# Sixteen rounds of adaLN modulation computed as row sums on VectorE in a two-layer diffusion trunk

## The chip, the cores and the metric

The kernel runs on one core of a Trainium2 chip. The metric is the device time of one execution in microseconds (us), as the median over the runs shown. Engines are named as the profile names them: PE is TensorE (its matmuls), PEld its weight loads, DVE is VectorE, ACT is ScalarE, POOL is GpSimd, and SP is SyncE, whose queue issues the loads of weights.

## The reference, cut to what matters

The model has two layers of three sub-layers each (FFN, token mixing, FFN), so six sub-layers, numbered 0 to 5 here. 128 context tokens and 256 latent tokens of width 1024 pass through all of them. Each sub-layer is modulated by three vectors of 1024 values, for each of two conditions (context and latent): a shift, a scale and a gate. These 18 vectors ("rounds") are what the change is about. A round is a 2 x 1024 by 1024 x 1024 product, with a weight of 4 MB.

```python
def trunk(x, cond, ...):
    for l in range(DEPTH):                                   # 2 layers
        m = (jax.nn.silu(cond) @ mod_w[l] + mod_b[l]).reshape(cond.shape[0], N_MOD, D_MODEL)   # 9 vectors
        g = norm_w[l]
        hf = modulate_norm(x, g[0], m[:, 0], m[:, 1])        # rms_norm(x, g) * (1 + scale) + shift
        x = x + FFN_RES * m[:, 2, None] * rms_norm(swiglu(hf, ffn_w1[l, 0], ffn_w2[l, 0]), g[1])
        hm = modulate_norm(x, g[2], m[:, 3], m[:, 4])
        out = mixer(hm)                                      # layer 0: "even", layer 1: "odd"
        x = x + m[:, 5, None] * rms_norm(out, g[3])
        hf = modulate_norm(x, g[4], m[:, 6], m[:, 7])
        x = x + FFN_RES * m[:, 8, None] * rms_norm(swiglu(hf, ffn_w1[l, 1], ffn_w2[l, 1]), g[5])
```

## The kernel before, in words

**Weights.** All weights of projections and all modulation weights form one stream of units of 128 x 2048 float32 (1 MB), in an order that `plan` (L1312) writes out. `load_upto` (L113) issues them on SP's queue into four buffers, `raw` (RAW_BUFS, L31). A weight unit consists of two halves. `prep` (L121) splits each half exactly into two float32r parts, `whi` (a copy on ACT, L150) and `wlo` (a subtraction on DVE, L153). After the second half's split the unit's `raw` buffer is given back and the next unit of the stream is loaded into it (L160 to L162). Three split halves exist at a time (HALF_BUFS), and `half` (L176) prepares two halves ahead of the one that TensorE uses. Every product is three matmuls (`mm3`, L456 to L458).

**An FFN** (`ffn`, L590) takes 22 units `w1` (each two halves of 24 matmuls over 384 columns), evaluates SiLU and the product (`gate_up`, L619 to L621, L442, L443) after each, and then runs `down` (L462) with 11 units `w2` (22 chunks of 18 matmuls over 512 columns). `down` ends token tile by token tile. At the boundary to the next sub-layer (`rest`, L548) the last tile's residual, norm, transposition and modulation run on DVE and ACT, while TensorE starts the next projection with the first two tiles (`early`, then the transposes of tile 2, then `late`). Between `order_begin` and `order_end` all engines issue in program order. Only the projections and the attention of the two mixers lie outside.

**Modulation.** The first two rounds are computed at the start (`start`, L723), in both kernels in the same way. Of the other 16:

- Ten rounds run on VectorE (`mod_dve`, L223). A unit holds 256 rows of the weight, with the contraction on the partitions. Four "pieces" per unit (two blocks of 128 rows by two conditions) multiply 1024 outputs by a scalar per partition and add them to `macc` (L241, L243). After the fourth unit TensorE sums over the partitions with a vector of ones (L253, 8 matmuls). The row result goes through DVE and two transposes (L295) into vectors, or, for a gate, through DRAM to all partitions.
- Six rounds run on TensorE (`mod_pe`, L198), 8 matmuls of 256 columns for each unit (L211). For five of them, the gates of sub-layers 1 to 5, three units are the "fill" that `rest` emits at the boundary ahead of the sub-layer (L549, L550), and the fourth comes a little later. The sixth, the scale of sub-layer 2, runs inside the even mixer.

The pieces wait in a list. `emit_pieces` (L265) emits two of them after each half of `w1` (L716). In `down` it divides what is left over the chunks (L487). MOD_PLAN (L1292) says which rounds are computed in which sub-layer and how many of their units lie among the first projection's, and `spread` (L1304) places them. `macc` has one buffer, which also serves as a spare pair of weight halves at each boundary (L166).

Of the kernel before, what the change touches and what calls it, by code (L numbers as in the profile page):

```python
# [16 lines left out]
ALU = mybir.AluOpType  # L17
# [19 lines left out]
class Trunk:  # L37
    def __init__(self, ctx, tc, io):
# [19 lines left out]
        self.mbT = const("mbT", [P, 6, 2, KC])  # L58
        nc.gpsimd.dma_start(self.mbT, io["mod_bT"])
        self.sel = const("sel", [P, 2])  # L60
# [6 lines left out]
        self.ones = const("ones", [P, 2, 32])  # L67
        nc.vector.memset(self.ones, 0.0)
        for c in range(2):
            nc.vector.memset(self.ones[:, c, c : c + 1], 1.0)  # L70
        self.xh = self.cp.tile([P, KC, TOK], F32R, tag="xh", name="xh")
        self.xl = self.cp.tile([P, KC, TOK], F32R, tag="xl", name="xl")
        self.gates, self.shift, self.scale = {}, {}, {}

# [117 lines left out]

    def mod_begin(self, r, bank):
        if r % 3 == 2:
            self.mod_aux = self.sp.tile([P, 512], F32, tag="maux", name=self.name("maux"), bufs=1)
            self.nc.sync.dma_start(self.mod_aux, self.io["mod_aux"][r // 3])

    def mod_pe(self, key, bank):  # L198
        """One unit of a round on the tensor engine, in four column groups."""
        _, r, u = key  # L200
        i = self.use(key)
        self.load_upto(i)
        raw, _ = self.raw.pop(i)
        self.load_upto(i + RAW_BUFS)
        if u == 0:
            self.mod_begin(r, bank)
            self.mod_ps = self.psum(bank)
        for kk in range(2):
            k = 2 * u + kk
            for g in range(4):  # L210
                self.nc.tensor.matmul(  # L211
                    self.mod_ps[32 * g : 32 * g + 32, 0:256], self.csT[:, k, :],
                    raw[:, kk * D + 256 * g : kk * D + 256 * (g + 1)],
                    start=(k == 0), stop=(k == KC - 1),
                )

    def mod_unit(self, key, bank):
        self.mod_pe(key, bank)
        if key[2] == 3:
            self.mod_rows(key[1])  # L220
            self.mod_finish(key[1], bank)

    def mod_dve(self, key):  # L223
# [3 lines left out]
        i = self.index[key]  # L227

        def piece(kk, c):
            def run():  # L230
                if kk == c == 0:
                    self.use(key)
                    self.load_upto(i)
                    if u == 0:
                        self.mod_begin(r, self.dve_bank)
                        self.mod_acc = self.cp.tile([P, 2, D], F32, tag="macc", name=self.name("macc"))
                k = 2 * u + kk
                w = self.raw[i][0][:, kk * D : (kk + 1) * D]
                acc, sc = self.mod_acc[:, c, :], self.csT[:, k, c : c + 1]
                if k == 0:  # L240
                    nc.vector.tensor_scalar(acc, w, sc, None, op0=ALU.mult)  # L241
                else:
                    nc.vector.scalar_tensor_tensor(acc, w, sc, acc, op0=ALU.mult, op1=ALU.add)  # L243
                if kk == c == 1:
                    del self.raw[i]
                    self.load_upto(i + RAW_BUFS)
            return run

        def reduce():
            self.mod_ps = self.psum(self.dve_bank)  # L250
            for c in range(2):
                for g in range(4):
                    nc.tensor.matmul(  # L253
                        self.mod_ps[32 * g : 32 * g + 32, 0:256], self.ones[:, c, :],
                        self.mod_acc[:, c, 256 * g : 256 * (g + 1)], start=(c == 0), stop=(c == 1),
                    )
            self.mod_rows(r)

        def finish():
            self.mod_finish(r, self.dve_bank)  # L260

        reduce.wait, finish.wait = True, False
        return [piece(kk, c) for kk in range(2) for c in range(2)] + ([reduce, finish] if u == 3 else [])
# [14 lines left out]
    def mod_vec(self, kind):  # L278
        return self.sp.tile([P, 2, KC], F32, tag=("shift", "scale")[kind], name=self.name("mv"))

    def mod_rows(self, r):
        self.mod_row = self.sp.tile([P, 256], F32, tag="mrow", name=self.name("mrow"), bufs=1)
        if r % 3 < 2:
            self.nc.vector.tensor_copy(self.mod_row, self.mod_ps[:, 0:256])
        else:
            self.nc.vector.tensor_tensor(self.mod_row, self.mod_ps[:, 0:256], self.mod_aux[:, 0:256], ALU.add)

    def mod_finish(self, r, bank):
        nc = self.nc
        s, kind = divmod(r, 3)  # L290
        rows = self.mod_row
        if kind < 2:
            tp = self.psum(bank)
            for j in range(2):
                self.transpose(tp[:, j * P : (j + 1) * P], rows[:, j * P : (j + 1) * P])  # L295
            res = self.mod_vec(kind)
            for j in range(2):
                src = tp[:, j * P : (j + 1) * P].rearrange("p (g c) -> p c g", c=32)[:, 0:2, :]
                dst = res.rearrange("p c (g j) -> p c g j", j=2)[:, :, :, j]
                per = lambda v: v.rearrange("p (g j) -> p g j", j=2)[:, :, j].unsqueeze(1).to_broadcast([P, 2, 4])  # L300
                nc.vector.tensor_tensor(dst, src, per(self.mbT[:, s, kind, :]), ALU.add)
                if kind == 1:
                    nc.vector.tensor_tensor(dst, dst, per(self.nwT[:, s, :]), ALU.mult)
            (self.shift if kind == 0 else self.scale)[s] = res
        else:
            half = 1.0 if s in (1, 4) else 0.5
            nc.vector.scalar_tensor_tensor(rows, rows, half, self.mod_aux[:, 256:512], op0=ALU.mult, op1=ALU.mult)
            scr = self.dp.tile([2, 4, 256], F32, tag="gscr", name=self.name("gscr"), bufs=2)
            for c in range(2):
                nc.gpsimd.dma_start(scr[c], rows.rearrange("(g c) n -> g c n", c=32)[:, c, :])  # L310
            gate = self.cp.tile([P, 2, D], F32, tag="gate", name=self.name("gate"))
            nc.gpsimd.dma_start(
                gate.rearrange("p c d -> p (c d)"),
                scr.rearrange("c g n -> (c g n)").partition_broadcast(P),
            )
            self.gates[s] = gate

# [28 lines left out]
    def square_steps(self, srcs):  # L346
        """The mean of squares of two halves, the second one first, as steps; and where the sums are."""
# [10 lines left out]
    def post_steps(self, t, acc, s):  # L358
        """x += gate * rms_norm(acc): steps for the second half, for the first half, and the update."""
# [26 lines left out]
    def stat_steps(self, t):  # L386
        """xn = -2 * x * rstd(x); the factor is made good in the scale."""
# [25 lines left out]
    def evac_steps(self, t, tp, s):  # L413
        """xh + xl = xn^T * scale + shift"""
# [31 lines left out]
    def order_begin(self):  # L446
        """From here to order_end the engines issue in the order of the program."""
# [1008 lines left out]
```

## Time and profile before

| | us |
|---|---|
| runs shown | 1457.07, 1460.22, 1461.21 |
| median | 1460.22 |
| span of the profiled execution (first to last instruction) | 1456.7 |

The profile gives the span of its execution, from the first instruction to the last. What lies around the span in that execution isn't listed apart. The three runs lie 0.4 to 4.5 us above the span, the median 3.5 us. The core's mean granted TensorE clock is 0.998 of full speed. The span divides into: the start and the first FFN (0 to 309 us), the even mixer (to 480), two FFNs (to 766 and 1050), the odd mixer (to 1172) and the last FFN.

In the profile, busy time is the time in which an engine had an instruction of its own in work, and "idle before" is the time that an engine stood still just before a group, with the instruction that released it. Matmuls overlap, so the distance between starts, not the duration, is what one costs TensorE. The same holds for VectorE, whose instructions overlap by less than 0.1 us. The profile counts a float32 matmul of L211, L253 or of a sum as two instructions.

### The profile page before, as it was taken

How to read it: one execution, taken by the hardware profiler on the slowest of the kernel's cores; microseconds unless marked ns; L12 is line 12 of the kernel's file. 1: busy time of each engine (PE TensorE's matmuls, PEld its weight loads, DVE VectorE, ACT ScalarE, POOL GpSimd, SP SyncE). 2: the span in 40 equal slices, each digit the busy share in tenths (PEclk: the TensorE clock that was granted, in tenths of full speed). 3: DMA queues.
4: the chain of work that ended last, by engine and by line, in shares of the span. 5: the costliest groups of instructions: out<-in, count | busy, mean ns of one | idle time of the engine just before them, and what ended most of it. 6: DMA issues, size and time to landing. Idle time of an engine off the chain costs nothing.

```text
span 1456.7 us, 20527 instructions
## 1 busy us (share of the span) xinstructions
PE 1442.6 (99%) x8305; PEld 1304.5 (90%) x8305; DVE 901.9 (62%) x1453; ACT 612.3 (42%) x1020; POOL 29.2 (2%) x53
## 2 busy tenths in 40 slices
PE   8999999999999999999999999999999999999998
PEld 6999998879888999998889999988876799999886
DVE  5778767474776657667656576674668764444333
ACT  5433332463555633332345333323547663333332
POOL 0000000010000000000000000000100000000000
PEclk9999999999999999999999999999999999999999
DMA  9565565645543464455535454555371345333331
GB/s 372 203 229 221 186 229 203 231 159 187 189 167 145 158 225 175 174 195 200 212 116 210 182 194 177 207 199 184 117 267 73 116 163 191 116 129 131 116 116 44
DMA packets 39232, 258.91 MB, mean 178 GB/s; under 512 B 5040, under 2 KB 5120, under 8 KB 9696
## 3 DMA queue, kind: packets, MB, share of 16 engines
q1 hardware_dynamic: 36288, 244.87, 45.7%
q0 software_dynamic: 2848, 12.72, 2.5%
q8 instruction: 65, 1.06, 0.3%
q14 instruction: 31, 0.25, 0.1%
HBM read 255.29 MB, written 2.28 MB: 177 GB/s over the span
## 4 chain that ended last, share of the span: by engine, by line
PE 97%; DMA 1%; ACT 0%; DVE 0%; issue 0%; SPq 0%; DVEq 0%; ACTq 0%
PE psB L456 30%; PE psB L457 30%; PE psB L458 30%; PE psB L405 2%; PE psB L939 2%; PE psB L211 1%; PE psB L980 1%; DMA raw<-in_mod_w 1%; PE psB L253 1%; PE psB L786 0%; DMA x<-in_x_prompt 0%; PE psB L953 0%; PE psB L799 0%; ACT junk L352 0%; PE psB L1263 0%
## 5 line engine op out<-in xcount | busy, mean ns | idle before, releaser
L456 PE MATMUL psB<-xh,whi 128*128 128x384 f32 (+1 forms) x1536 | 517.6, 337 | 0.2 <-ACT xh L442 0.2
L457 PE MATMUL psB<-xl,whi 128*128 128x384 f32 (+1 forms) x1536 | 512.3, 334 | 0.2 <-DVE xl L443 0.2
L458 PE MATMUL psB<-xh,wlo 128*128 128x384 f32 (+1 forms) x1536 | 512.1, 333 | 0.0
L153 DVE TENSOR_TENSOR wlo<-raw,whi 128x1024 fp32r<-128x1024 f32 (+2 forms) x286 | 336.8, 1186 | 175.1 <-ACT whi L150 172.0
L150 ACT CAST whi<-raw 128x1024 fp32r<-128x1024 f32 (+1 forms) x275 | 286.5, 1045 | 341.8 <-PE psB L457 173.9
L456 PEld LDWEIGHTS psB<-xh,whi 128*128 128x128 f32 x1536 | 288.7, 188 | 8.7 <-issue 6.0
L457 PEld LDWEIGHTS psB<-xl,whi 128*128 128x128 f32 x1536 | 288.9, 188 | 1.1 <-DVE xl L443 0.7
L458 PEld LDWEIGHTS psB<-xh,wlo 128*128 128x128 f32 x1536 | 288.7, 188 | 0.0
L243 DVE SCALAR_TENSOR_TENSOR macc<-raw,csT,macc 128x1024 f32<-128x1024 f32 x140 | 173.8, 1279 | 0.0
L456 PE MATMUL psB<-whi,g 128*128 128x512 f32 x384 | 150.3, 391 | 0.0
L457 PE MATMUL psB<-wlo,g 128*128 128x512 f32 x384 | 149.6, 389 | 0.0
L458 PE MATMUL psB<-whi,g 128*128 128x512 f32 x384 | 149.5, 389 | 0.0
L621 DVE TENSOR_TENSOR gt<-psB,sil 128x384 f32<-128x384 f32 (+1 forms) x88 | 48.2, 548 | 131.5 <-PE psB L458 129.5
L442 ACT CAST g<-gt 128x384 fp32r<-128x384 f32 (+1 forms) x84 | 42.4, 505 | 175.8 <-DVE gt L621 175.8
L456 PEld LDWEIGHTS psB<-whi,g 128*128 128x128 f32 x384 | 72.1, 188 | 15.9 <-issue 1.2
L458 PEld LDWEIGHTS psB<-whi,g 128*128 128x128 f32 x384 | 72.1, 188 | 15.1
L457 PEld LDWEIGHTS psB<-wlo,g 128*128 128x128 f32 x384 | 72.1, 188 | 14.5
L619 ACT ACTIVATE sil<-psB 128x384 f32<-128x384 f32 (+1 forms) x88 | 42.7, 485 | 90.3 <-PE psB L458 90.3
L443 DVE TENSOR_TENSOR g<-gt,g 128x384 fp32r<-128x384 f32 (+1 forms) x84 | 46.1, 549 | 48.0 <-ACT g L442 48.0
L456 PE MATMUL psB<-g,g 128*128 128x512 f32 x120 | 46.9, 391 | 0.0
L458 PE MATMUL psB<-g,g 128*128 128x512 f32 x120 | 46.7, 390 | 0.0
L457 PE MATMUL psB<-g,g 128*128 128x512 f32 x120 | 46.7, 389 | 0.0
(229 smaller groups left out, 1461.1 us busy)
## 6 DMA issues: line engine op xcount, KB each, us to landing
raw<-in_ffn_w SPq DMA_DIRECT2D x129, 1024.0 KB, 4.8
raw<-in_mod_w SPq DMA_DIRECT2D x64, 1024.0 KB, 5.1
raw<-in_ev_in SPq DMA_DIRECT2D x10, 1024.0 KB, 5.4
m<-in_mod_first SPq DMA_DIRECT2D x8, 1024.0 KB, 13.0
gate<-gscr POOLq DMA_DIRECT2D x6, 1024.0 KB, 5.7
raw<-in_ev_out SPq DMA_DIRECT2D x4, 1024.0 KB, 4.8
raw<-in_od_out SPq DMA_DIRECT2D x4, 1024.0 KB, 5.4
bias<-in_rpb POOLq DMA_DIRECT2D x8, 384.0 KB, 4.0
```

Of the source, the lines that this page charges most:

```text
L150: nc.scalar.copy(hi, src)
L153: sub = lambda hi=hi[:, c], lo=lo[:, c], src=src[:, c]: nc.vector.tensor_tensor(lo, src, hi.bitcast(F32), ALU.subtract)
L243: nc.vector.scalar_tensor_tensor(acc, w, sc, acc, op0=ALU.mult, op1=ALU.add)
L405: self.nc.tensor.transpose(out, src, self.ident)
L442: self.nc.scalar.copy(hi, src)
L443: sub = lambda: self.nc.vector.tensor_tensor(lo, src, hi.bitcast(F32), ALU.subtract)
L456: nc.tensor.matmul(out, ah, bh, start=first, stop=False)
L457: nc.tensor.matmul(out, ah, bl, start=False, stop=False)
L458: nc.tensor.matmul(out, al, bh, start=False, stop=last)
L619: nc.scalar.activation(sil[:, :n], pg[:, :n], AF.Silu)
L621: nc.vector.tensor_tensor(gt[:, :n], pu[:, :n], sil[:, :n], ALU.mult)
L939: nc.tensor.matmul(sp[:, :384], qk(i, e, t + 1), kk(i, e)[0], start=True, stop=True)
```

## The change

The modulation weight is laid out transposed in DRAM: a unit now holds 256 outputs, with the outputs on the partitions and the 1024 contraction elements along the free axis. A piece becomes one `tensor_tensor_reduce` on VectorE: it multiplies 128 x 1024 weights by the conditioning vector, which stands on all partitions (`csB`, 1 MB for both conditions), sums along the free axis, starts from the bias and writes one column of the result vector. All 16 rounds take this way, 256 pieces in all. The sum over partitions, its row copies, the two transposes per shift or scale, and all modulation matmuls of these rounds are gone. A gate's vector takes one transpose of 16 columns, a copy, a write to DRAM and a load to all partitions (`gate_load`), which is issued behind `rest`.

`csB` lives in the buffer of `macc`. It is loaded anew in each sub-layer that computes rounds: the first time from the input with a SiLU on ScalarE, then from DRAM. The rounds are computed in the order 2 to 17: five in sub-layer 0, one in the even mixer (one piece after each half), five in sub-layer 2, four in sub-layer 3, none in 4, one in 5. Nothing is emitted at a boundary any more.

The diff, cut to its core (docstrings and comments are also gone, `ones` becomes one column, arguments named `fill` disappear everywhere):

```diff
+    def mod_cond(self, first):
+        nc = self.nc
+        self.csB = self.cp.tile([P, 2, D], F32, tag="macc", name=self.name("csB"))
+        flat = self.csB.rearrange("p c d -> p (c d)")
+        if first:
+            nc.gpsimd.dma_start(flat, self.io["cond_rows"].partition_broadcast(P))
+        else:
+            nc.gpsimd.dma_start(flat, self.cond_rows.rearrange("c d -> (c d)").partition_broadcast(P))
+
+    def mod_cond_ready(self):
+        nc = self.nc
+        if self.cond_rows is None:
+            flat = self.csB.rearrange("p c d -> p (c d)")
+            nc.scalar.activation(flat, flat, AF.Silu)
+            self.cond_rows = self.dp.tile([2, D], F32, tag="crows", name="crows")
+            nc.gpsimd.dma_start(self.cond_rows.rearrange("(o c) d -> o (c d)", o=1), flat[0:1, :])
...
                     if u == 0:
-                        self.mod_begin(r, self.dve_bank)
-                        self.mod_acc = self.cp.tile([P, 2, D], F32, tag="macc", name=self.name("macc"))
+                        self.mod_res = self.mod_vec(kind)
                 k = 2 * u + kk
-                w = self.raw[i][0][:, kk * D : (kk + 1) * D]
-                acc, sc = self.mod_acc[:, c, :], self.csT[:, k, c : c + 1]
-                if k == 0:
-                    nc.vector.tensor_scalar(acc, w, sc, None, op0=ALU.mult)
-                else:
-                    nc.vector.scalar_tensor_tensor(acc, w, sc, acc, op0=ALU.mult, op1=ALU.add)
+                junk = self.cp.tile([P, D], BF16, tag="junkv", name=self.name("junkv"))
+                nc.vector.tensor_tensor_reduce(
+                    junk, self.raw[i][0][:, kk * D : (kk + 1) * D], self.csB[:, c, :], 1.0,
+                    self.mbT[:, s, kind, k : k + 1], ALU.mult, ALU.add, self.mod_res[:, c, k : k + 1])
                 if kk == c == 1:
                     del self.raw[i]
                     self.load_upto(i + RAW_BUFS)
+                    if u == 3:
+                        self.mod_done(s, kind)
             return run
-        def reduce():
...
+        def rows():
+            self.mod_gate_rows(s, self.dve_bank)
+        rows.wait = True
+        return [piece(kk, c) for kk in range(2) for c in range(2)] + ([rows] if u == 3 and kind == 2 else [])
+
+    def mod_gate_rows(self, s, bank):
+        tp = self.psum(bank)
+        self.transpose(tp[0:16, 0:P], self.mod_res.rearrange("p c k -> p (c k)"))
+        rows = self.sp.tile([16, P], F32, tag="grow", name=self.name("grow"), bufs=1)
+        nc.vector.tensor_copy(rows, tp[0:16, 0:P])
+        scr = self.dp.tile([16, P], F32, tag="gscr", name=self.name("gscr"), bufs=2)
+        nc.gpsimd.dma_start(scr, rows)
+        self.gate_rows[s] = scr
+        if s == self.sub:
+            self.gate_load(s)
...
-        def rest(early, late, fill):
-            for key in fill:
-                self.mod_unit(key, 3)
+        def rest(early, late):
             second, first, update = post[2]
...
-            rest(early, late, fill)
+            rest(early, late)
+        self.gate_ready()
         self.dve_bank = 2
         pieces = []
         ahead = p1[p1.index(units[done]) + 1 :]
-        for key in units[done:]:
-            on_pe = []
+        for n, key in enumerate(units[done:]):
+            if n == 1:
+                self.mod_cond(s == 0)
             while ahead and ahead[0][0] == "mod":
-                k = ahead.pop(0)
-                if k[1] in PE_ROUNDS:
-                    on_pe.append(k)
-                else:
-                    pieces += self.mod_dve(k)
+                pieces += self.mod_pieces(ahead.pop(0))
...
-                self.emit_pieces(pieces, 2)
-            for k in on_pe:
-                self.mod_unit(k, 3)
+                if n and pieces:
+                    self.mod_cond_ready()
+                    self.emit_pieces(pieces, 2)
...
         for key in p1:                                       (even mixer)
             if key[0] == "mod":
-                self.mod_unit(key, 3 if key[1] in PE_ROUNDS else 7)
+                if not pieces and key[2] == 0:
+                    self.mod_cond(False)
+                pieces += self.mod_pieces(key)
...
                 evac[kind](j, ps)
+                self.emit_pieces(pieces, 1)
+        while pieces:
+            self.emit_pieces(pieces, 1)
...
-        mods = [k for k in p1 if k[0] == "mod"]              (odd mixer)
-        for k in mods:
-            self.mod_unit(k, 3)
...
 MOD_PLAN = [
-    ([(0, 2), (1, 0), (1, 1), (2, 0)], 12, None),
-    ([(2, 1)], 4, (1, 2)),
-    ([(3, 0), (3, 1), (4, 0)], 8, (2, 2)),
-    ([(4, 1), (5, 0), (5, 1)], 8, (3, 2)),
-    ([], 0, (4, 2)),
-    ([], 0, (5, 2)),
+    (range(2, 7), 15), (range(7, 8), 4), (range(8, 13), 15), (range(13, 17), 12), ((), 0), (range(17, 18), 4),
 ]
```

In MOD_PLAN a round is (sub-layer, 0 shift / 1 scale / 2 gate) before, and three times the sub-layer plus that kind after. The number behind it is how many of the units lie among the first projection's.

## Rows read from the trace of the kernel before

**Rows 1.** The page: busy time of each engine, and the chain by engine.
```profile
PE 1442.6 (99%) x8305; PEld 1304.5 (90%) x8305; DVE 901.9 (62%) x1453; ACT 612.3 (42%) x1020; POOL 29.2 (2%) x53
PE 97%; DMA 1%; ACT 0%; DVE 0%; issue 0%; SPq 0%; DVEq 0%; ACTq 0%
```

**Rows 2.** Windows: length, busy (count) of PE, PEld, DVE, ACT, POOL; PEclk, DMA share, GB/s.
```profile
53.50:215.00 161.50, 161.50 (x961) 158.92 (x961) 122.16 (x138) 59.76 (x81) 1.74 (x3) 1.00 0.58 210
370.00:430.00 60.00, 60.00 (x385) 50.23 (x384) 48.03 (x124) 31.97 (x74) 2.81 (x6) 1.00 0.47 164
```

**Rows 3.** TensorE's timeline: start, us, line; w1 pace, w2 pace, sum, transposes, unit.
```profile
55.09 0.33 PE L456 MATMUL psB<-xh,macc 128*128 128x384 f32 x1
...
57.69 0.34 PE L456 MATMUL psB<-xh,whi 128*128 128x384 f32 x1
...
103.54 1.07 PE L253 MATMUL psB<-macc,ones 128*32 128x256 f32 x16
104.54 0.45 PE L456 MATMUL psB<-xh,whi 128*128 128x384 f32 x1
...
270.02 0.38 PE L405 MATMUL psB<-ident,mrow 128*128 128x128 f32 x2
...
270.48 0.39 PE L457 MATMUL psB<-wlo,g 128*128 128x512 f32 x1
...
271.63 0.39 PE L456 MATMUL psB<-whi,g 128*128 128x512 f32 x1
...
278.43 0.39 PE L456 MATMUL psB<-g,g 128*128 128x512 f32 x1
...
405.60 1.07 PE L211 MATMUL psB<-raw,csT 128*32 128x256 f32 x16
406.60 0.59 PE L939 MATMUL psB<-kT,qz 128*128 128x384 f32 x1
```

**Rows 4.** Timelines of TensorE and ScalarE at the boundaries to sub-layers 1 and 4.
```profile
308.90 2.80 PE L211 MATMUL psB<-raw,csT 128*32 128x256 f32 x48
311.63 0.50 PE L456 MATMUL psB<-whi,xh 128*128 128x512 f32 x1
...
316.72 0.72 ACT L399 ACTIVATE xn<-x,rz 128x512 f32<-128x512 f32 x1 [0.68 <-DVE rz L343]
...
317.34 1.09 PE L405 MATMUL psB<-ident,xn 128*128 128x128 f32 x8
...
1056.85 0.73 ACT L399 ACTIVATE xn<-x,rz 128x512 f32<-128x512 f32 x1 [0.68 <-DVE rz L343]
...
1058.16 1.03 PE L405 MATMUL psB<-ident,xn 128*128 128x128 f32 x8
```

**Rows 5.** TensorE's timeline in the odd mixer, with the idle time before the unit.
```profile
1063.29 0.40 PE L211 MATMUL psB<-raw,csT 128*32 128x256 f32 x1 [1.82 <-DMA raw<-in_mod_w]
```

**Rows 6.** Groups by line: busy us, mean ns of one | idle before, releaser.
```profile
L153 DVE TENSOR_TENSOR wlo<-raw,whi 128x1024 fp32r<-128x1024 f32 (+2 forms) x286 | 336.8, 1186 | 175.1 <-ACT whi L150 172.0
L150 ACT CAST whi<-raw 128x1024 fp32r<-128x1024 f32 (+1 forms) x275 | 286.5, 1045 | 341.8 <-PE psB L457 173.9
L243 DVE SCALAR_TENSOR_TENSOR macc<-raw,csT,macc 128x1024 f32<-128x1024 f32 x140 | 173.8, 1279 | 0.0
L352 ACT ACTIVATION_READ_ACCUMULATOR junk<-psB 128x1 f32 x36 | 7.1, 198 | 0.0
```

**Rows 7.** VectorE's timeline among the w1 units of sub-layer 0.
```profile
123.18 2.47 DVE L243 SCALAR_TENSOR_TENSOR macc<-raw,csT,macc 128x1024 f32<-128x1024 f32 x2
125.58 1.21 DVE L153 TENSOR_TENSOR wlo<-raw,whi 128x1024 fp32r<-128x1024 f32 x1
126.71 2.47 DVE L243 SCALAR_TENSOR_TENSOR macc<-raw,csT,macc 128x1024 f32<-128x1024 f32 x2
```

**Rows 8.** The page's DMA issues, and SP's waits (us in total, times, longest).
```profile
raw<-in_ffn_w SPq DMA_DIRECT2D x129, 1024.0 KB, 4.8
...
SPq L117 <- DVE wlo L153: 817.3, 131, 13.9
```

More of the change, by code (lines that the diff above doesn't have):

```diff
@@ L66, in __init__ @@
         make_identity(nc, self.ident)
[L67 to L70, printed above, removed]
+        self.one = const("one", [P, 1])
+        nc.vector.memset(self.one, 1.0)
         self.xh = self.cp.tile([P, KC, TOK], F32R, tag="xh", name="xh")
@@ L189, in release, with mod_pieces @@
         self.live.discard((self.index[key], h))
[L193 to L223, printed above, removed]
+    def mod_cond(self, first):
[13 more added lines that the diff above has]
+            nc.gpsimd.dma_start(self.cond_rows.rearrange("(o c) d -> o (c d)", o=1), flat[0:1, :])
+    def mod_pieces(self, key):
         nc = self.nc
@@ L265, in emit_pieces, with gate_load, gate_ready @@
+    def gate_load(self, s):
+        gate = self.cp.tile([P, 2, D], F32, tag="gate", name=self.name("gate"))
+        self.nc.gpsimd.dma_start(gate.rearrange("p c d -> p (c d)"),
+                                 self.gate_rows.pop(s).rearrange("k p -> (k p)").partition_broadcast(P))
+        self.gates[s] = gate
+    def gate_ready(self):
+        if self.sub in self.gate_rows:
+            self.gate_load(self.sub)
     def emit_pieces(self, pieces, n):
@@ L278, in mod_vec @@
     def mod_vec(self, kind):
[L279 to L284, printed above, removed]
-        else:
[L286 to L316, printed above, removed]
+        return self.sp.tile([P, 2, KC], F32, tag=("shift", "scale", "gatev")[kind], name=self.name("mv"))
     def rstd_of(self, ss, n=1, ss2=None, between=None):
@@ L481, in down @@
         self.dve_bank = 0
-        pieces += [f for k in keys if k[0] == "mod" for f in self.mod_dve(k)]
+        pieces += [f for k in keys if k[0] == "mod" for f in self.mod_pieces(k)]
         for c in range(nmain):
@@ L754, in start @@
                 first = self.sp.tile([P, 1], F32, tag="l", name=self.name("l"), bufs=4)
-                nc.scalar.activation(first, self.ones[:, 0, 0:1], func)
+                nc.scalar.activation(first, self.one, func)
                 if func == AF.Silu:
@@ L990, in attention_steps, with mixer @@
             yield
-    def mixer(self, s, p1, p2, fill, rest):
+    def mixer(self, s, p1, p2, rest):
         es, ea = ExitStack(), ExitStack()
@@ L998, in mixer @@
         self.more_pool = lambda e, n: pool(e, n)
-        (self.even if s == 1 else self.odd)(p1, fill, rest, pool(ea, "att"), mh, ml)
+        (self.even if s == 1 else self.odd)(p1, rest, pool(ea, "att"), mh, ml)
         ea.close()
@@ L1035, in late @@
                 self.prep(1)
-        rest(early, late, fill)
+        rest(early, late)
+        self.gate_ready()
         for k, h in halves[len(ws):]:
@@ L1054, in proj_tile, with even @@
         return ps
-    def even(self, p1, fill, rest, mp, mh, ml):
+    def even(self, p1, rest, mp, mh, ml):
         nc, io = self.nc, self.io
@@ L1070, in even @@
         units = [k for k in p1 if k[0] == "ev_v"]
-        vps = self.moving_first(units, 2, 512, [(0, 512)], [(0,), (1,), (7,)], rest, fill)
+        vps = self.moving_first(units, 2, 512, [(0, 512)], [(0,), (1,), (7,)], rest)
         self.order_end()
@@ L1144, in even, with odd @@
                 evac[kind](j, ps)
+                self.emit_pieces(pieces, 1)
+        while pieces:
+            self.emit_pieces(pieces, 1)
         for _ in att:
             pass
[L1148 removed]
+    def odd(self, p1, rest, mp, mh, ml):
         nc, io = self.nc, self.io
@@ L1169, in odd @@
         units = [k for k in p1 if k[0] == "od_qkv"]
-        acc = self.moving_first(units, 1, 768, [(0, 512), (512, 768)], [(0, 1), (6, 7), (4, 5)], rest, fill)
+        acc = self.moving_first(units, 1, 768, [(0, 512), (512, 768)], [(0, 1), (6, 7), (4, 5)], rest)
         for a in range(2):
@@ L1343, in build @@
     tr.half_alloc[tr.index["w1", 0, 3], 0] = tr.spare_half
-    for p1, _, _ in phases[1:]:
+    for p1, _ in phases[1:]:
         tr.half_alloc[tr.index[p1[0]], 1] = tr.spare_half
     rest = None
-    for s, (p1, p2, fill) in enumerate(phases):
-        rest = (tr.mixer if s % 3 == 1 else tr.ffn)(s, p1, p2, fill, rest)
+    for tr.sub, (p1, p2) in enumerate(phases):
+        rest = (tr.mixer if tr.sub % 3 == 1 else tr.ffn)(tr.sub, p1, p2, rest)
     tr.order_end()
```

68 lines of the change are left out of this document (31 added, 37 removed).

## The prediction, made blind

> **What bounds the kernel now.** I read the page's busy times first, then the chain of waits, then windows, timelines and DMA issues. TensorE is busy 99% of the span, and 97% of the chain lies on it, with nothing for VectorE and 1% for DMA [rows 1]. In sub-layer 0's first projection TensorE is busy for all of its 161.5 us, VectorE for 122.2, at full clock [rows 2]. So whatever TensorE no longer does is gained, as long as weights reach it as early as now. Two places where that might fail have to be read: the boundaries, and the stretches where modulation shares VectorE and the weight stream with the projection.
>
> The pace to beat: 15 matmuls of a w1 unit start in 2.60 us [rows 3], so a unit of 48 takes 8.3 us; in the output projection 30 take 6.80 us, so a w2 unit of 36 takes 8.2 us.
>
> **What the change removes.** The sum over partitions takes 1.0 us from its start to the next matmul (103.54 to 104.54), ten times: 10.0 us. A pair of transposes takes 270.02 to 270.48, less the 0.23 us of one matmul: 0.24 us, ten times: 2.4 us. A modulation unit on TensorE takes 1.0 us (405.60 to 406.60) [rows 3]. Nine of the 24 such units lie outside the boundaries: 9.0 us. In the odd mixer TensorE also waited 1.8 us for such a unit's load [rows 5], which goes.
>
> The other 15 units, three at each of five boundaries, I cost at nothing. At 308.90 they take 2.73 us. Then come two parts of the next projection, and tile 2's transposes at 317.34. These need tile 2's normalised rows, whose second half ScalarE ends at 316.72 + 0.72 = 317.44 [rows 4]; the transposes of that half come last. That chain runs on VectorE and ScalarE from the transposes of tile 1 and from tile 2's last product, both ahead of the fill, so it doesn't get shorter. Without the fill TensorE waits where it worked: 13.7 us of work go, and 13.7 us of waits come, less 0.6 at sub-layer 4 (1057.58 against 1058.16). That the boundaries give all 13.7 us is excluded by this chain.
>
> Six gate transposes are added, 0.2 us each like half a pair with its start: 1.2 us. The gain on TensorE is 10.0 + 2.4 + 9.0 + 1.8 + 0.6 - 1.2 = 22.6 us.
>
> **What it adds.** VectorE gets 256 pieces where it had 160. Two old pieces take 125.58 - 123.18 = 2.40 us, 1.20 each, and a split's subtraction 1.13 [rows 7]. The trace before has no multiply with a row sum. Below, 1.13: it reads two tensors as the subtraction does. Above, for an engine that gives out its sum apart: 1.20 + 0.20, ScalarE's accumulator read [rows 6]. I take 1.30, the middle. The old piece, which reads two float32 tensors from SBUF, takes 1279 ns for 1024 elements, against 1186 in the mean for a subtraction [rows 6].
>
> [...]
>
> Now the load in sub-layers 0 and 2. Per w1 unit VectorE does two subtractions (2.3 us) and the two gating operations with the wait between them (1.6 us): 3.9 of 8.3. Fifteen units over 18 positions are 3.3 pieces per w1 unit, 4.3 us more; in sub-layer 2 fifteen over 16, 4.9 us. That is 8.2 and 8.8 us: VectorE is full. It would be a small loss if that were all.
>
> What decides is the **weight stream**. Four raw buffers carry it, and SP waited 817 us for subtractions to free one, as it should when loads are early [rows 8]. A modulation unit keeps its buffer until its fourth piece is emitted, and the emission is at most four pieces per w1 unit. Going through the list by hand: in sub-layer 0 pieces begin one w1 unit late (n = 1) while the first modulation unit is already listed, and a gate's `rows` entry costs turns. So after each of the w1 units 3 to 13 at least four pieces are left: one whole unit in arrears. In sub-layer 2 the arrears come with the first gate's entry and last from unit 9 to unit 19. In sub-layer 3 (12 units, 16 positions) they pass at once. A unit in arrears means that three of the four buffers hold modulation (one in work, one waiting, one loaded ahead), and the w1 units go through a single one. Then nothing overlaps any more:
>
> - load of a w1 unit: 4.8 us to landing [rows 8], 0.1 for the semaphore
> - copy of its first half 1.05 us [rows 6], subtraction 1.2 with its semaphore
> - two pieces that VectorE's queue has next: 2.6
> - subtraction of the second half, which frees the buffer: 1.2.
>
> 10.95 us against TensorE's 8.3: 2.6 us lost per w1 unit. The copies and gating fit in between. The halves split ahead absorb three or four of the eleven units. Sub-layer 0: 7.5 x 2.6 = 19.5; sub-layer 2: 8.5 x 2.6 = 22. In `down` after them five modulation units lie among the first w2 units, 2 pieces per chunk, with the same cycle: about three w2 units lose 2.8 each: 8.4, twice. Together 28 + 30.5 = 58.5 us. Before, 12 and 8 units lay there and the arrears stayed under one unit.
>
> The even mixer: in 370 to 430 us VectorE is busy 48.0 of 60 [rows 2]. Ten pieces of 1.30 come, 1.5 us of row copies go: 59.5, where TensorE without its units would need 56. Softmax steps wait for matmuls and exponentials in between, so I add 4 us of idle: a loss of 7.5, say 8 with the two pieces outside the window. Between 5 (VectorE bound exactly there goes unnoticed) and 13.
>
> At nothing: the four later loads of `csB` and the gate loads on POOL's queue. They carry 1 MB each and are issued more than a w1 unit before their first reader, which covers them; uncovered, each costs about 5 us like a weight load [rows 8]. The first `csB` waits until TensorE has read `macc` (57.69 [rows 3]), then for its load (about 5) and the SiLU over 2048 columns on ScalarE (two copies, 2.1): 65, where VectorE could start at about 62. VectorE's queue, gating and subtractions behind it, stands for these 3 us. The next two halves are split by then, and cover it; otherwise it costs 3.
>
> **The sum.** Gain 22.6, losses 58.5 + 8 = 66.5: 43.9 us more. On the span, 1456.7 + 43.9 = 1500.6; on the median, which lies 3.5 above it, **1504 us**. Bounds: with pieces of 1.13, one w1 unit of slack more and 5 us less in the even mixer, about 20 us more: 1480. With 1.40 and half a microsecond more per load, 15 us in the FFNs and 5 in the mixer on top, then other traffic on the loads: 1540.
>
> **Rivals.**
>
> - *The stream doesn't starve.* If the arrears stay under one unit, the w1 units keep two buffers, the cycle above spreads over two units (5.5 us each), and VectorE at 8.2 to 8.8 us per unit costs a few tenths. Then the gain stands: 1460 - 22.6 = 1438 us. For it: SP's waits are for VectorE, not for the wire, and no copy waits for a load in this profile. Against: the count of the list. It decides at four pieces left over at the end of a w1 unit.
> - *The loss is about the gain.* The halves split ahead absorb more than I think, or loads land sooner; the losses come to 20 to 45 us. Then the time is 1456 to 1480 us, mostly a little slower.
> [...]
>
> **How the numbers follow.** The forecast's mechanism rests on a count of the program and on durations in rows, so it gets 0.76, all of it slower. The stream that doesn't starve gets 0.10, loss about equal to gain 0.09 (within the bound 0.03, faster 0.01, slower 0.05), half rate 0.05. The runs shown differ by 0.3%, so 0.3%, 4.4 us, is about what a measurement can tell. Faster 0.11, same 0.03, slower 0.86. The range takes the first case with both ends and the slower part of the third: 1467 to 1545 us.
>
> **What would show it.** In the profile after: no L211, no sum over partitions; pieces of 1.2 to 1.4 us back to back; in sub-layer 0 from about its third w1 unit, and in the second half of sub-layer 2's, TensorE idle 2 to 3 us per unit, ended by the subtraction, with ScalarE's copies waiting for the DMA of `raw` (before: only for TensorE); sub-layers 3 and 5 without such gaps and 5 and 1 us shorter; TensorE waiting some 2.7 us in total at each boundary. Loads that never keep a copy waiting would refute the single buffer; idle time of TensorE behind pieces alone would make VectorE's rate the cause. [...]

## The result, and the profile after

The changed kernel takes **1503.07 us** (median; 1500.93 to 1505.33), the kernel before 1458.64 (1456.81 to 1461.21) in the same comparison: a ratio of 1.031, 95% interval 1.029 to 1.033. The forecast was 1504. The profiled span went from 1456.7 to 1501.4, 44.7 us more.

The page after, busy times, then the chain by engine and by line (against [rows 1]):

```profile
PE 1442.7 (96%) x7747; PEld 1308.3 (87%) x7747; DVE 1022.8 (68%) x1768; ACT 609.8 (41%) x1021; POOL 29.0 (2%) x54
PE 66%; DVE 13%; DMA 9%; ACT 6%; issue 5%; DVEq 0%; ACTq 0%; SPq 0%
PE psB L435 20%; PE psB L436 20%; PE psB L437 20%; DMA raw<-in_ffn_w 8%; DVE junkv L229 5%; DVE wlo L155 4%; ACT whi L152 2%; ACT junk L331 2%; PE psB L384 2%; PE psB L914 1%; DMA raw<-in_mod_w 1%; PE psB L955 1%; DVE x L361 1%; DVE xl L422 1%; ACT xh L421 0%
```

TensorE held 97% of the chain before and holds 66% now. Over half of the rest, 19%, lies on three links that take turns: the load of a weight unit (8%), row sums (5%) and splits (4 + 2%). VectorE, which took the work over, is far from full: it is busy 68%.

Groups by line after (busy, mean of one | idle before, releasers), then SP's waits (us in total, times, longest):

```profile
L229 DVE CUSTOM_DVE_ANT_0 junkv<-raw,csB,mbT 128x1024 bf16<-128x1024 f32 x256 | 328.1, 1281 | 13.0 <-DMA raw<-in_mod_w 8.2 <-ACT csB L209 0.6
L229 DVE DVE_READ_ACCUMULATOR2_ANT mv<- 128x1 f32 x256 | 21.2, 83 | 0.0
L152 ACT CAST whi<-raw 128x1024 fp32r<-128x1024 f32 (+1 forms) x275 | 282.9, 1044 | 352.3 <-DMA raw<-in_ffn_w 143.8 <-PE psB L436 99.3 <-PE psB L437 98.3
```
```profile
SPq L119 <- DVE wlo L155: 928.8, 131, 37.8
SPq L119 <- DVE mv L229: 191.7, 52, 8.7
```

ScalarE's copies waited only for TensorE before; now 143.8 us of their idle time end with the DMA of a weight unit. The load itself is no slower: on the page after it lands after 4.8 us in the median, as before [rows 8].

A w1 unit of sub-layer 2 in arrears, from VectorE's, ScalarE's and SP's timeline, and the gaps of TensorE in the same stretch:

```profile
607.59 0.33 SPq L119 DMA_DIRECT2D raw<-in_ffn_w  x1
...
611.72 0.33 SPq L119 DMA_DIRECT2D raw<-in_mod_w  x1
612.56 1.99 ACT L152 CAST whi<-raw 128x1024 fp32r<-128x1024 f32 x2 [3.99 <-DMA raw<-in_ffn_w]
613.64 1.23 DVE L155 TENSOR_TENSOR wlo<-raw,whi 128x1024 fp32r<-128x1024 f32 x1 [1.95 <-ACT whi L152]
...
614.78 1.28 DVE L229 CUSTOM_DVE_ANT_0 junkv<-raw,csB,mbT 128x1024 bf16<-128x1024 f32 x1
...
616.11 1.28 DVE L229 CUSTOM_DVE_ANT_0 junkv<-raw,csB,mbT 128x1024 bf16<-128x1024 f32 x1
...
617.32 1.22 DVE L155 TENSOR_TENSOR wlo<-raw,whi 128x1024 fp32r<-128x1024 f32 x1
```
```profile
618.57 0.33 SPq L119 DMA_DIRECT2D raw<-in_ffn_w  x1
...
629.35 0.33 SPq L119 DMA_DIRECT2D raw<-in_ffn_w  x1
```
```profile
613.66 0.45 PE L435 MATMUL psB<-xh,whi 128*128 128x384 f32 x1 [1.33 <-ACT whi L152]
...
614.92 0.44 PE L437 MATMUL psB<-xh,wlo 128*128 128x384 f32 x1 [0.64 <-DVE wlo L155]
```

Here the forecast's cycle can be read off. The load is issued at 607.59 and lands after 4.9 us. ScalarE can copy at 612.56, after 4.97 us. The first subtraction runs at 613.64, two row sums at 614.78 and 616.11 (1.33 us apart), the second subtraction from 617.32. With its end the buffer is free, and the next load is issued at 618.57, 10.98 us after the last one; the one after it follows in 10.78. The forecast said 10.95.

The boundaries, from the transposes of tile 1 to those of tile 2, after and before (windows: length, busy (count) of PE, PEld, DVE, ACT, POOL; PEclk, DMA share, GB/s):

```profile
317.88:337.74 19.86, 17.05 (x84) 13.84 (x82) 15.57 (x45) 13.27 (x33) 6.19 (x8) 1.00 0.24 84
486.14:505.99 19.85, 17.89 (x108) 15.23 (x106) 15.20 (x44) 13.28 (x33) 0.00 (x0) 1.00 0.00 0
801.18:821.30 20.12, 17.91 (x107) 15.21 (x106) 15.19 (x44) 13.26 (x33) 0.55 (x1) 1.00 0.14 53
1083.06:1104.59 21.53, 19.41 (x96) 16.39 (x95) 16.11 (x45) 13.88 (x34) 5.75 (x10) 0.92 0.31 106
1203.09:1222.93 19.84, 17.86 (x107) 15.19 (x105) 15.18 (x44) 13.27 (x33) 0.00 (x0) 1.00 0.00 1
```
```profile
297.48:317.34 19.86, 19.86 (x132) 15.29 (x130) 15.58 (x45) 13.28 (x33) 5.63 (x7) 1.00 0.37 138
468.54:488.49 19.95, 19.95 (x155) 16.66 (x154) 15.28 (x44) 13.37 (x33) 0.00 (x0) 1.00 0.33 124
753.10:773.05 19.95, 19.95 (x156) 16.66 (x155) 15.28 (x44) 13.38 (x33) 0.00 (x0) 1.00 0.33 126
1037.62:1058.16 20.54, 20.54 (x144) 16.46 (x142) 15.30 (x44) 13.76 (x34) 5.18 (x9) 1.00 0.33 95
1160.00:1179.96 19.96, 19.96 (x156) 16.66 (x155) 15.31 (x44) 13.38 (x33) 0.00 (x0) 1.00 0.32 124
```

Without the fill TensorE works 17 to 18 us in such a stretch instead of 20, and the stretch is as long as before. The one to sub-layer 4 (21.53 us) is the exception: a lower clock lies in it. The starts of these windows also cut the run into six stages (the last one ends with the span):

| sub-layer | before | after | difference |
|---|---|---|---|
| 0 | 297.5 | 317.9 | +20.4 |
| 1, even mixer | 171.1 | 168.3 | -2.8 |
| 2 | 284.6 | 315.0 | +30.5 |
| 3 | 284.5 | 281.9 | -2.6 |
| 4, odd mixer | 122.4 | 120.0 | -2.4 |
| 5 | 296.7 | 298.3 | +1.6 |

The loss lies in the two sub-layers that take five rounds. Two things were not in the forecast's sum. In sub-layers 3 and 5, where nothing waits, most w1 units now take 8.48 us where they took 8.32 (TensorE's timeline after, the first matmuls of two units in a row):

```profile
876.08 0.34 PE L435 MATMUL psB<-xh,whi 128*128 128x384 f32 x1
...
884.56 0.34 PE L435 MATMUL psB<-xh,whi 128*128 128x384 f32 x1
```

And the granted clock, full all along before but for the run's last microseconds, fell to 0.50 of full speed in stretches of 34 us in all, most of them in the starved part of the two sub-layers. Windows of sub-layer 2: the whole starved stretch, and one such fall in it with the time ahead of it:

```profile
594.70:709.60 114.90, 102.10 (x529) 96.85 (x529) 87.84 (x128) 31.65 (x44) 0.00 (x0) 0.94 0.58 200
```
```profile
613.66:624.45 10.79, 8.87 (x49) 8.22 (x49) 8.39 (x13) 2.90 (x5) 0.00 (x0) 1.00 0.54 193
624.45:626.80 2.35, 1.71 (x8) 1.39 (x9) 2.35 (x3) 1.28 (x2) 0.00 (x0) 1.00 0.90 383
626.80:630.20 3.40, 3.40 (x13) 3.40 (x12) 2.95 (x6) 0.38 (x1) 0.00 (x0) 0.50 0.00 0
```

From 613.66 to 624.45 TensorE was busy 8.87 of 10.79 us, with a gap of 0.64 us in it and one of 1.28 at its end, and a second gap of 0.64 follows. In the 3.40 us at the lower clock 11 matmuls start (13 are in work), where 19 start at full clock.

### The profile page after: what moved, and what is told of

Its sections match the earlier page's. It is cut to its first block, busy times and chain, and to the rows that moved or that the text cites. A ratio compares the mean times of both kernels' runs of the same rounds, so it can differ in the third digit from the quotient of the medians.

```text
span 1501.4 us, 19747 instructions
## 1 busy us (share of the span) xinstructions
PE 1442.7 (96%) x7747; PEld 1308.3 (87%) x7747; DVE 1022.8 (68%) x1768; ACT 609.8 (41%) x1021; POOL 29.0 (2%) x54
## 3 DMA queue, kind: packets, MB, share of 16 engines
q1 hardware_dynamic: 35424, 243.29, 44.7%
## 4 chain that ended last, share of the span: by engine, by line
PE 66%; DVE 13%; DMA 9%; ACT 6%; issue 5%; DVEq 0%; ACTq 0%; SPq 0%
PE psB L435 20%; PE psB L436 20%; PE psB L437 20%; DMA raw<-in_ffn_w 8%; DVE junkv L229 5%; DVE wlo L155 4%; ACT whi L152 2%; ACT junk L331 2%; PE psB L384 2%; PE psB L914 1%; DMA raw<-in_mod_w 1%; PE psB L955 1%; DVE x L361 1%; DVE xl L422 1%; ACT xh L421 0%
## 5 line engine op out<-in xcount | busy, mean ns | idle before, releaser
L437 PE MATMUL psB<-xh,wlo 128*128 128x384 f32 (+1 forms) x1536 | 519.4, 338 | 10.0 <-DVE wlo L155 10.0
L436 PE MATMUL psB<-xl,whi 128*128 128x384 f32 (+1 forms) x1536 | 517.8, 337 | 1.2 <-DVE ss L333 0.7
L152 ACT CAST whi<-raw 128x1024 fp32r<-128x1024 f32 (+1 forms) x275 | 282.9, 1044 | 352.3 <-DMA raw<-in_ffn_w 143.8
L229 DVE CUSTOM_DVE_ANT_0 junkv<-raw,csB,mbT 128x1024 bf16<-128x1024 f32 x256 | 328.1, 1281 | 13.0 <-DMA raw<-in_mod_w 8.2
L435 PE MATMUL psB<-whi,g 128*128 128x512 f32 x384 | 152.1, 396 | 6.8 <-ACT whi L152 6.8
L437 PE MATMUL psB<-whi,g 128*128 128x512 f32 x384 | 151.2, 394 | 0.0
## 6 DMA issues: line engine op xcount, KB each, us to landing
m<-in_mod_first SPq DMA_DIRECT2D x8, 1024.0 KB, 12.7
```

What stands on the lines that cost most here:

```text
L152: nc.scalar.copy(hi, src)
L229: nc.vector.tensor_tensor_reduce(junk, self.raw[i][0][:, kk * D : (kk + 1) * D], self.csB[:, c, :], 1.0, self.mbT[:, s, kind, k : k + 1], ...
L435: nc.tensor.matmul(out, ah, bh, start=first, stop=False)
L436: nc.tensor.matmul(out, ah, bl, start=False, stop=False)
L437: nc.tensor.matmul(out, al, bh, start=False, stop=last)
```

## The experiments

Three questions were open: whether the single buffer or VectorE's rate costs the time; what the lower clock adds; and where 8.48 us come from.

**Three pieces after each half.**

```diff
-                    self.emit_pieces(pieces, 2)
+                    self.emit_pieces(pieces, 3)
```

> Up to three pieces instead of two after each half of w1; the same 256 pieces, in the same order, and nothing else changed. Single-buffer theory: the list takes 6 pieces per w1 unit where 3.3 are supplied, so less than a unit is ever in arrears, the w1 units keep two raw buffers, no ACT copy waits for a load of in_ffn_w, and the granted clock stays full in sub-layers 0 and 2. Over their undisturbed pace (8.48 and 8.16 us) the w1 and w2 units of sub-layers 0 and 2 lost 23 + 33 = 56 us; nearly all of it comes back: 1445 to 1453 us. VectorE-rate theory (it has too much work per unit, in whatever order): the work is the same, so the time stays within 10 us of 1503, with TensorE waiting for subtractions.

Measured: 1470.67 us, ratio 1.008 (1.006 to 1.010). 32 of the 56 us came back, so neither expectation holds alone. In sub-layer 0's projection one stall is left and the units behind it take 8.38 us instead of up to 11.1. In sub-layer 2 one stall is left too, but the units then take 8.9. The w2 units 3 to 5 (counted from 0) of both sub-layers still lost 6.5 and 8 us (6.4 and 9.2 in the changed kernel). The granted clock, expected to be full in both sub-layers, was not: it rose from 0.987 to 0.993 in the mean. ScalarE's copies still wait 84.2 us for loads, not 143.8:

```profile
L152 ACT CAST whi<-raw 128x1024 fp32r<-128x1024 f32 (+1 forms) x275 | 283.9, 1044 | 314.5 <-PE psB L436 117.9 <-PE psB L437 103.5 <-DMA raw<-in_ffn_w 84.2
```

Two remainders were to be explained: `down`, and the 8.9 us.

**The same, with the last modulation units spread over 8 positions of w2 instead of 6.**

```diff
-        phases.append((b1, spread(b2, ext[n1:], 0, 6)))
+        phases.append((b1, spread(b2, ext[n1:], 0, 8)))
```

> As the run with three pieces after each half, and besides the last modulation units of sub-layers 0 and 2 stand among the first 8 positions of the w2 stream instead of 6 (the same pieces). Single-buffer theory: in that run the w2 units 3 to 5 lost 6.5 and 8 us because modulation units held three of the four raw buffers; spread thinner, most of it comes back: 1456 to 1461 us. Rival (VectorE has too many pieces there, since as many pieces are emitted per chunk): within 3 us of 1470.7.

Measured: 1455.72 us, ratio 0.9986 (0.9976 to 0.9995), 15 us less than without it. The w2 units 3 to 5 take 8.16 us, and the copies wait 29.7 us for loads:

```profile
L152 ACT CAST whi<-raw 128x1024 fp32r<-128x1024 f32 (+1 forms) x275 | 284.5, 1044 | 289.3 <-PE psB L437 138.6 <-PE psB L436 114.8 <-DMA raw<-in_ffn_w 29.7
```

As many pieces are emitted after each chunk; only the order of the stream differs. That settles `down` for the single buffer.

What is left in sub-layer 2 is **VectorE's rate**. SP's queue and the window of that stretch, in this kernel:

```profile
609.56 0.33 SPq L119 DMA_DIRECT2D raw<-in_ffn_w  x1
...
618.51 0.33 SPq L119 DMA_DIRECT2D raw<-in_ffn_w  x1
...
627.45 0.33 SPq L119 DMA_DIRECT2D raw<-in_ffn_w  x1
```
```profile
602.20:664.20 62.00, 59.78 (x333) 57.52 (x332) 57.41 (x85) 19.58 (x28) 0.00 (x0) 1.00 0.63 233
```

Loads follow each other every 8.95 us, and VectorE is busy 57.41 of 62 us: two subtractions (2.3), four row sums (5.1; 1.33 us each, or 1.21 where a subtraction follows) and the gating with its wait (1.6) make up the 8.95. The changed kernel itself runs at this pace at the end of sub-layer 0's projection, once the arrears no longer hold the third buffer: its loads come 8.95 us apart there too.

**Spare matmuls in the gaps**, to keep the clock up.

```diff
+            if (s == 0 and 4 <= n <= 12) or (s == 2 and n >= 10):
+                spare = self.psum(3)
+                for _ in range(8):
+                    nc.tensor.matmul(spare[:, 0:TOK], self.xh[:, 0, 0:P], self.xh[:, 0, :], start=True, stop=True)
```

> The changed kernel with 8 spare matmuls of 384 columns (1.4 us) ahead of each w1 unit in the starved stretches (9 units of sub-layer 0, 10 of sub-layer 2); their results go nowhere. Single-buffer theory: the load cycle sets the period, so it stays 10.8 to 11.0 us, the spare work fits into the idle time, the clock stays full in these stretches, and the time is within 5 us of 1503. Clock theory (six of the ten stretches of 3.4 us at the lower clock lie there and cost half of their length): about 10 us less, 1493. Work theory (TensorE has no slack there): 19 x 1.4 = 27 us more, 1530.

Measured: 1498.83 us, ratio 1.028 (1.026 to 1.030). 27 us of work were added and the time fell by 4. The window of sub-layer 2's projection from its first starved unit on, and SP's queue in it:

```profile
594.70:706.90 112.20, 108.88 (x608) 105.76 (x608) 88.79 (x129) 31.79 (x44) 0.00 (x0) 1.00 0.57 199
```
```profile
616.26 0.33 SPq L119 DMA_DIRECT2D raw<-in_ffn_w  x1
...
627.30 0.33 SPq L119 DMA_DIRECT2D raw<-in_ffn_w  x1
...
638.15 0.33 SPq L119 DMA_DIRECT2D raw<-in_ffn_w  x1
```

At full clock, and with TensorE busy 97%, the loads still come 10.85 to 11.04 us apart. The load's cycle sets the period, not TensorE; the work theory is out. The stages of sub-layers 0, 2 and 4 got 0.6, 4.8 and 1.0 us shorter. The 4.8 us do not show a cost of the lower clock. In the changed kernel three weight loads of sub-layer 2, issued at 594.54, 640.34 and 728.54, took 6.9, 6.2 and 6.5 us to land, some 5 us more than three loads of 4.8; with the spare matmuls no weight load there took more than 5.0. The second of the three, in the changed kernel:

```profile
640.34 0.33 SPq L119 DMA_DIRECT2D raw<-in_ffn_w  x1
...
646.65 2.00 ACT L152 CAST whi<-raw 128x1024 fp32r<-128x1024 f32 x2 [5.32 <-DMA raw<-in_ffn_w]
...
647.74 0.69 PE L435 MATMUL psB<-xh,whi 128*128 128x384 f32 x1 [2.80 <-ACT whi L152]
...
652.65 0.33 SPq L119 DMA_DIRECT2D raw<-in_ffn_w  x1
```

TensorE's unit ahead of this copy takes 12.31 us, the one behind it, with the longest of the low stretches in it, 11.78, and the third 9.97: 34.1 in all, 1.4 more than three cycles of 10.9, and by 1.4 us the load was late. Why such loads land late stays open. The 1.0 us at sub-layer 4 are the clock's: the boundary's window there takes 20.38 us instead of 21.53, at full clock.

**Where tiles lie.** The constants ahead of `xh` have other sizes in the changed kernel, so that `xh` and the tiles behind it start at a multiple of 64 bytes within a partition; before, they start 32 bytes beyond one. Two kernels swap that.

```diff
-        self.one = const("one", [P, 1])
+        self.one = const("one", [P, 9])[:, 0:1]
```

> The changed kernel with the constant behind ident padded from 4 to 36 bytes per partition, so that xh, xl, whi, wlo and all tiles behind it lie 32 bytes higher, at the same offset within 64 bytes as in the kernel before. Address theory: the w1 unit goes back from 8.48 to 8.32 us wherever TensorE sets the pace (some 70 of 88 units): 11 us less, 1492 us; starved units keep their period of 10.8 to 11.0 us. Rival, that the slower pace comes from other traffic (pieces, loads, writes of junkv): 8.48 stays, 1503 us.

Measured: 1496.17 us, ratio 1.026 (1.024 to 1.028). Units of sub-layers 2, 3 and 5 take 8.32 us, those of sub-layer 0 still 8.48.

```diff
-        self.ones = const("ones", [P, 2, 32])
+        self.ones = const("ones", [P, 72])[:, 0:64].rearrange("p (c n) -> p c n", c=2)
```

> The kernel before with its vector of ones padded by 32 bytes per partition, so that xh and what follows lie at the changed kernel's offset within 64 bytes; no other edit. Address theory: all 88 w1 units go from 8.32 to 8.48 us, 14 us more: 1473 us. Rival (other traffic): 8.32 stays, 1459 us.

Measured: 1458.84 us, ratio 1.0007 (0.9993 to 1.0022): 8.32 us in all undisturbed units. So the address alone is not the cause, and neither is other traffic alone, since the first of the two kernels has the same traffic. The address theory fits three FFNs of the first kernel and falls with the second; its rival falls with the first. What the units had in common was another thing: once entered, a pace (8.32, 8.38 or 8.48) lasted until the next interruption of the train of matmuls.

**Float32 matmuls ahead of the train**, as modulation on TensorE had put them there.

```diff
+            if n == 0:
+                spare = self.psum(3)
+                for g in range(4):
+                    nc.tensor.matmul(spare[32 * g : 32 * g + 32, 0:256], self.csT[:, 0, :], self.x[:, 0, 0:256],
+                                     start=True, stop=True)
```

> The changed kernel with four spare float32 matmuls of 256 columns (about 0.5 us) behind the first unit of each FFN's loop, as modulation on TensorE put them there before; their results go nowhere. Theory that the pace of a train of w1 matmuls is set by how it was entered: the units behind it go from 8.48 to 8.32 us in sub-layers 2, 3 and 5 until the next interruption, some 8 us less: 1495 us. Rival (other traffic, or where tiles lie): 8.48 stays, 1504 us.

Measured: 1497.65 us in a single run. TensorE's timeline in sub-layer 3 of this kernel, the first matmul of a unit and of the next but one:

```profile
866.53 0.34 PE L435 MATMUL psB<-xh,whi 128*128 128x384 f32 x1
...
883.17 0.34 PE L435 MATMUL psB<-xh,whi 128*128 128x384 f32 x1
```

16.64 us for two units: 8.32 each, with the addresses and the traffic of the changed kernel. In sub-layer 3 the stage takes 280.2 us instead of 281.9, in sub-layer 5 296.8 instead of 298.3, spare matmuls included. The last run below shows 8.32 in these sub-layers too. In sub-layer 3 the pace depends on how the train is entered: 8.32 us behind the float32 matmuls, 8.48 without them. Why there are three paces stays open.

**The even mixer without its row sums.**

```diff
-                pieces += self.mod_pieces(key)
+                i = self.use(key)
+                self.load_upto(i)
+                del self.raw[i]
+                self.load_upto(i + RAW_BUFS)
+                self.scale[2] = self.shift[2]
```

> The changed kernel without the 16 row sums of the even mixer: their weights are loaded and not read, and sub-layer 2 takes its shift for its scale, so that the round of the scale is left out. The stage from tile 1's transposes at its beginning to those at its end takes 168.3 us with them. Prediction's term: the full VectorE costs 8 us there (5 to 13): 160 us (155 to 163). Rival, from the stage's time before (171.1) and the TensorE work that left it (five units and a pair of transposes, 5.7 us): the pieces cost 2.9: 165.4 us. The whole time falls by as much, 1495 or 1500 us.

Measured: its stage runs from the transposes at 316.95 to those at 481.60 us, 164.65 instead of 168.26. The 16 pieces cost 3.6 us there, near the rival's 2.9 and below the forecast's 8, and also below its lower bound of 5. The whole time was 1496.54 us in a single run.

**The gates back on TensorE**, as fill at the boundaries; the other eleven rounds stay row sums. To make room, the squares' junk tile shares the pieces' one, and a gate's rows are finished in the tile of its constants.

```diff
 MOD_PLAN = [
-    (range(2, 7), 15), (range(7, 8), 4), (range(8, 13), 15), (range(13, 17), 12), ((), 0), (range(17, 18), 4),
+    ((2, 3, 4, 6), 12, None), ((7,), 4, 5), ((9, 10, 12), 8, 8), ((13, 15, 16), 8, 11), ((), 0, 14), ((), 0, 17),
 ]
+FILL = 3
+PE_ROUNDS = {p[2] for p in MOD_PLAN if p[2]}
...
         def rest(early, late):
+            for key in self.fill:
+                self.mod_unit(key, 3)
...
+            for k in on_pe:
+                self.mod_unit(k, 3)
```

> The gates of sub-layers 1 to 5 are computed on TensorE again as in the kernel before (three units as fill at each boundary, the fourth in the next projection); the other eleven rounds are row sums on VectorE, with 12, 8 and 8 of their units among the first projections of sub-layers 0, 2 and 3. Single-buffer theory: less than a unit is in arrears, so no ACT copy waits long for a load, and TensorE keeps the gain: against the kernel before 10 sums of 1.1 us, 9 pairs of transposes of 0.34 and about 1.8 in the even mixer go, 0.2 for a transpose comes: 16 us less, 1442 us, or 1456 if a w1 unit takes 8.48 instead of 8.32 us. The boundaries take 19.9 us from the transposes of tile 1 to those of tile 2 with and without fill. VectorE-rate theory (a row sum costs too much beside the splits): units of 8.9 us and more remain in sub-layers 0 and 2: 1465 or more.

Measured: **1440.91 us, ratio 0.988 (0.986 to 0.990)**: faster than both kernels. The page's busy times and chain, and the window of the first boundary:

```profile
PE 1425.8 (99%) x8062; PEld 1299.1 (90%) x8062; DVE 928.9 (65%) x1608; ACT 612.7 (43%) x1021; POOL 31.9 (2%) x58
PE 96%; DVE 2%; DMA 1%; ACT 1%; issue 0%; DVEq 0%; SPq 0%; ACTq 0%
```
```profile
292.94:312.80 19.86, 19.86 (x131) 15.29 (x130) 15.58 (x45) 13.27 (x33) 5.62 (x7) 1.00 0.36 123
```

TensorE is the bound again. The fill is back in the boundary, which takes 19.86 us for the third time: 19.86 with it before, 19.86 without it after, 19.86 with it here.

**All 16 rounds on VectorE, with the three remedies** (three pieces, 8 positions, float32 matmuls) and 13 instead of 15 units in sub-layer 2's projection.

> All 16 rounds on VectorE as in the changed kernel, with what the runs so far say against its losses: three pieces after each half, the last units among the first 8 positions of w2, 13 instead of 15 units among the projection of sub-layer 2 (so that VectorE has under four pieces per w1 unit), and four spare float32 matmuls behind the first unit of each FFN's loop. From 1455.7 us (the first two alone): 5 us less in sub-layer 2 (eight units of 8.95), and 5 to 7 us less for 8.32 instead of 8.48 or 8.38 us per w1 unit, less 2 for the spare matmuls: 1447 us, 1442 to 1452. Rival (VectorE cannot take 16 rounds at any spacing): 1455 or more.

Measured: 1450.34 us, ratio 0.994 (0.992 to 0.996). The window that was VectorE's at 8.95 us per unit now belongs to TensorE, with units of 8.32:

```profile
600.00:660.00 60.00, 60.00 (x348) 60.00 (x347) 53.44 (x77) 20.85 (x28) 0.00 (x0) 1.00 0.64 234
```

The seven units that now stand in sub-layer 2's `down` cost its w2 units 5 us in turn, and one stall of 3 us is left in sub-layer 0. So VectorE can take all 16 rounds. That is 9 us slower than with the gates at the boundaries, where they cost nothing.

## Why the prediction was right, point by point

The forecast was 43.9 us more on the span, 44.7 were measured. Its mechanism holds; four terms were off and cancel.

- **Weight stream**: 58.5 forecast. Over their undisturbed pace the units of sub-layers 0 and 2 lost 16.8 and 21.9 us in the projections (19.5 and 22 forecast) and 6.6 and 11.3 in `down` (8.4 each): 56.6. The cycle of 10.95 is there (10.8 to 11.1, and longer where a load lands late). In sub-layer 0 it began and ended later and was broken twice: from 70 to 168 us most weight loads are issued 10.8 to 12.3 us apart, but two pairs only 4.1. TensorE feels it from the unit that starts at 87; five units lose 2 to 3 us each, two between them next to nothing. The last seven lose 0.4 to 0.7 each to VectorE's rate, which the forecast took for next to nothing.
- **TensorE's gain**: 22.6 forecast, about 28 found. Read from whole units of before, a sum over partitions cost 1.10 us (9.42 against 8.32), not 1.0: 11.0. A pair of transposes cost 0.34 to 0.43, not 0.24: 3.7. A unit on TensorE cost 1.10 and delayed the matmuls behind it by 0.1 to 0.24 more: 11.5 for nine. With the 1.8 of the odd mixer that is 28. A gate's transpose costs under 0.1, not 0.2. The 0.6 at sub-layer 4 were 0.2.
- **Fill at nothing**: right. The windows above show it, and the run with the gates shows it from the other side. TensorE waits 2.81 us at once at the first boundary and 2.12 at the one to sub-layer 4; at the others 2.0 to 2.2 us fall into several gaps, the last one of 0.4. The boundary to sub-layer 4 took 21.53 us with a low clock in it (0.92 in the mean of the window); in the runs where the clock stayed full there it took 20.4, 1.1 less.
- **Even mixer**: 8 forecast, 3.6 measured. The step that failed is the 4 us of idle time added on top of a full VectorE: VectorE is busy 55.2 of 60 us there (385 to 445 us), and TensorE's gaps behind the boundary (0.36, 0.84 and 0.46 us) come to 1.7 us. The other 1.9 us lie in TensorE's busy time, 163.8 us in this stage against 161.8 without the row sums; how they arise stays open.
- **Pieces**: 1.30 taken, 1.33 measured: 1281 ns and an accumulator read of 83 ns, overlapping a little. Two float32 tensors from SBUF and a sum out take 1.33 us for 1024 elements, with the old piece at 1.20 and a subtraction at 1.13 [rows 7]. No run shows a row sum at half rate, to which the chances gave 0.05: the 256, a custom operation in the trace, take 1265 to 1286 ns each.
- **`csB` at nothing**: right. VectorE stood 0.59 us for the first SiLU, not 3, and the first row sum began at 65.99 us where the forecast had 65. The four later loads landed after 7.2 us in the median, not 5, and no row sum waited for them.
- **Left out**: the pace of 8.48. From the units that differ it comes to about 11.6 us over the four FFNs. Of these, 3 to 4 us lie in units of sub-layers 0 and 2 whose period the load or VectorE sets anyway. Counted over 8.32, as the forecast did, they belong to the stream, which then comes to about 60 and the pace to about 8. The lower clock was not in the sum either: 1.1 us at the boundary to sub-layer 4. Within the 56.6 no run shows a cost of it, while the three late loads make some 5 us of them.

Together: 56.6 + 3.6 + 11.6 + 1.1 - 28 = 44.9. Next to these, the forecast had the mixer 4.4 and the stream 1.9 too high and the gain 5.4 too low; the pace and the clock at one boundary, neither of them in the sum, made that good with 12.7. The step from the span to the median, 3.5 in the forecast, was 1.7 (1503.07 against 1501.4). So it is luck that the number came out closer than its terms. The mechanism was right on its own, as the runs with three pieces and with spare matmuls show.

Sub-layers 3 and 5 have no gaps, as said, but are 2.6 us shorter and 1.6 longer instead of 5 and 1 shorter, which is the pace again: with the float32 matmuls it is 4.3 shorter and 0.2 longer.

## What to carry to other kernels

Where one ring of buffers carries two streams, count how many of its buffers the slower consumer can hold at once. As soon as one buffer is left for the other stream, its load, its work and its release stop overlapping, and the period is their sum, although no engine is full (in the starved stretch above the period was mostly 10.8 to 11.0 us, with TensorE busy 102 of 115 us and VectorE 88). Order and rate of the consumer decide that: the same 256 row sums cost 45 us or nothing (1503.07 and 1455.72 us).

Work taken off the busiest engine pays only where this engine sets the end. Where it waits for another chain anyway, as at these boundaries (the first takes 19.86 us with the fill and without), work is free, and it is the right place for what would crowd another engine.

## What was not expected of the hardware

In these runs a train of 384-column matmuls kept one of three paces, 8.32, 8.38 or 8.48 us per 48, until something interrupted it. Four float32 matmuls ahead of it led to 8.32 in sub-layers 2, 3 and 5, and the train without them to 8.48 there. Moving `xh` and the tiles behind it by 32 bytes also led to 8.32 in three of four FFNs, but the opposite move changed nothing in the kernel before (8.32 us). The cause stays open.

The granted clock fell to 0.50 of full speed in the 3.40 us from 626.80 on; ahead of this fall TensorE had stood 1.28 and 0.64 us.
